# The MLP's input in one tile at an offset of its own, and a fifth room for the last gate's weight blocks

## The chip, the cores and the metric

The kernel runs on one core of one Trainium2 chip. The metric is the device time of one execution in microseconds; the median of three runs of the kernel before is 1739.65 us (1736.71 to 1743.08).

## The reference, cut to what matters

One layer of a diffusion backbone over 256 latent tokens and 256 context tokens of width 2048: an HGRN2 mixer, then a gated MLP with a width-3 convolution. The part that the change touches is the MLP on the latent tokens and the last of the six modulation vectors, the gate of the MLP:

```python
sh_ml, sc_ml, gt_ml, sh_fl, sc_fl, gt_fl = jnp.split((silu_c @ ada_w[i] + ada_b[i])[:, None, :], N_MOD, axis=-1)
h_l = modulate(rms_norm(x_lat, norm_ffn_pre[i]), sh_fl, sc_fl)
gate, up = jnp.split(h_l @ w_in, 2, axis=-1)          # 2048 -> 2 x 5632
f_l = (silu(dwconv_centred(gate, conv_w, conv_b)) * up) @ w_out
x_lat = x_lat + gt_fl * rms_norm(f_l, norm_ffn_post[i])
```

## The kernel before, in words

Every large product runs as three float32r matmuls (`mm3`, lines 200 to 202): an operand is split into a high part, rounded by a cast on ScalarE (line 106), and a low part, the difference, on VectorE (line 107). The three matmuls are high x high, high x low and low x high. The first operand of a matmul is stationary (its 128x128 block is loaded into TensorE), the second one moves past it, 256 or 512 columns at a time.

The weights stream through `Stream` (`ws`): blocks of 512 KB are loaded by SyncE's queue into four buffers `w_raw`, then split into three buffers each of `w_hi` and `w_lo`. A block of the MLP's first product has 4 x 2 stationary blocks, so it feeds 24 matmuls.

The stages in order: a start in which the modulation of the mixer is computed, the mixer's projections, its output product, a bridge in which the MLP's input is normed, turned and modulated, the MLP's first product with the convolution (22 steps of 8 weight blocks, lines 1063 to 1110), and the MLP's second product with the norm at its end.

The MLP's input is kept in 16 tiles, `h2h0` to `h2h7` (high parts) and `h2l0` to `h2l7` (low parts), each 128 partitions x 2 x 256 float32r, 2,048 bytes in a partition (lines 946 to 950). They move in the MLP's first product: one matmul reads one run of 256 numbers, 1,024 bytes, of one of them. The constant `SHIFT` (64) and the spacers of lines 531 and 947 place them: `w_hi` and `w_lo` start 64 bytes behind a multiple of 256 bytes of a partition, the `h2` tiles on a multiple of 256. In the mixer's projections with stationary weights the moving tiles `hTh`, `hTl` start on a multiple of 256 too; where the activations are stationary (the `v` projection and both output products) the weights move, and the moving side is the one 64 bytes behind. The tiles are filled by 8 casts and 8 subtractions (line 1062), and the first 64 float32 matmuls of the MLP (line 1077) read the unsplit copy `h2f`.

The last gate (`ada_part(5, ...)`, line 1058) needs a matrix-vector product with 2048 x 2048 numbers of `ada_w`. It is done beside the MLP's first 14 steps: 64 blocks of 256 KB are loaded by SyncE's queue (line 346) into a ring of `ADA_BUFS` = 4 tiles `ada_w`, and VectorE multiplies each by its number of the condition and adds it to one of four accumulators (lines 361 and 363). Three blocks are asked for ahead; after that each step of the generator asks for one more block and then uses one. The program places one such step per weight block, but the order of instructions on each engine is drawn up by the framework's planner, which fills idle time of its model with later work: the 64 loads are issued between 992.7 us and 1097.6 us of the span. VectorE and SyncE's queue run in that fixed order: a load of `ada_w` waits until its room is free (VectorE has used the block that lay there), a load of `w_raw` until the split of the block four earlier is done.

Of the kernel before, what the change touches and what calls it, by code (L numbers as in the profile page):

```python
# [8 lines left out]
F32 = mybir.dt.float32  # L9
F32R = mybir.dt.float32r  # L10
# [7 lines left out]
P = 128  # L18
D = 2048
KT = D // P  # L20
T = 256
# [8 lines left out]
MIX_RATE = 1.85  # L30
ADA_RATE = 3
ADA_BUFS = 4
ASIDE = 14


@with_exitstack
def tile_hgrn2_convffn_layer(
# [7 lines left out]
    ada_w, ada_b = ada_w[0], ada_b[0]  # L45
# [12 lines left out]
    def spacer(pool, nbytes):  # L58

        pool.tile([P, nbytes // 4], F32, name="spacer", bufs=1)  # L60
# [3 lines left out]
    SHIFT = 64  # L64
# [3 lines left out]
    def bank(pool, name):  # L68
        return pool.tile([P, 512], F32, name=name)
# [34 lines left out]
    def split(hi, lo, src):  # L104

        S.copy(out=hi, in_=src)  # L106
        V.tensor_tensor(out=lo, in0=src, in1=hi.bitcast(F32), op=ALU.subtract)  # L107

    class Stream:
# [37 lines left out]
        def next(self):  # L147
            self.ahead()
            got = self.done[self.pos]
            self.done[self.pos] = None  # L150
            self.pos += 1
            return got
# [186 lines left out]

    grow = {}  # L340

    def ada_part(part, pool):
        def loaded(i):
            b, r = divmod(i, KT)
            aw = pool.tile([P, 512], F32, name="ada_w", bufs=ADA_BUFS)
            nc.sync.dma_start(out=aw, in_=ada_w[r * P:(r + 1) * P, part * D + b * 512:part * D + (b + 1) * 512])
            return aw

        accs = []
        aws = [loaded(i) for i in range(ADA_BUFS - 1)]  # L350
        yield
        yield
        for b in range(4):
            acc = pool.tile([P, 512], F32, name="ada_acc", bufs=4)
            for r in range(KT):

                if len(aws) < 4 * KT:
                    aws.append(loaded(len(aws)))
                aw = aws[b * KT + r]
                if r == 0:  # L360
                    V.tensor_scalar(out=acc, in0=aw, scalar1=cst[:, r, 0:1], scalar2=None, op0=ALU.mult)
                else:
                    V.scalar_tensor_tensor(out=acc, in0=aw, scalar=cst[:, r, 0:1], in1=acc,  # L363
                                           op0=ALU.mult, op1=ALU.add)
                yield
            accs.append(acc)
        for _ in range(8):
            yield

        one = bank(ps_mi, "mi")  # L370
        for b in range(4):
            PE.matmul(out=one[32 * b:32 * b + 32, :], lhsT=ones32, rhs=accs[b], start=True, stop=True,
                      tile_position=(0, 32 * b), skip_group_check=True)
        strip_sb = pool.tile([P, 512], F32, name="ada_w", bufs=ADA_BUFS)
        S.copy(out=strip_sb, in_=one)
        for _ in range(4):
            yield
        if part in (3, 4):
            tp = bank(ps_mi, "mi")
            for i in range(4):  # L380
                PE.transpose(out=tp[:, i * P:(i + 1) * P], in_=strip_sb[:, i * P:(i + 1) * P], identity=ident)
            dst = shc_f if part == 3 else scc_f

            V.tensor_tensor(out=dst.rearrange("p (b i) -> p i b", i=4),
                            in0=tp.rearrange("p (i b r) -> p i b r", i=4, r=32)[:, :, :, 0],
                            in1=adab[:, part, :].rearrange("p (b i) -> p i b", i=4), op=ALU.add)
            if part == 4:
                V.scalar_tensor_tensor(out=scc_f, in0=scc_f, scalar=1.0, in1=g_ffn, op0=ALU.add, op1=ALU.mult)
        else:
            post = n_mix_post if part == 2 else n_ffn_post  # L390
            for w, src in enumerate((ada_b[part * D:(part + 1) * D], post[0])):
                gb = pool.tile([P, 512], F32, name="ada_acc", bufs=4)
                nc.gpsimd.memset(gb, 0.0)
                nc.sync.dma_start(out=gb[0::32, :], in_=src.rearrange("(b n) -> b n", b=4))
                V.tensor_tensor(out=strip_sb, in0=strip_sb, in1=gb, op=(ALU.add, ALU.mult)[w])
            gd = dram.tile([4, 512], F32, name=f"gd{part}")
            nc.sync.dma_start(out=gd, in_=strip_sb[0::32, :])
            grow[part] = gd
        yield
# [242 lines left out]
    def mixer():  # L642
        for p in range(NP):
            while "q" not in have.get(p, {}):
                yield
            yield from scan(p)
# [209 lines left out]
    def ada_rest():  # L856
        for part in (2, 3, 4):
            yield from ada_part(part, sp)

    ada, mix = ada_rest(), mixer()  # L860
# [66 lines left out]
    h2h, h2l, h2f, xin, hold = [], [], [], [], []  # L927

    def mixed():

        nonlocal h2
        with tc.high_priority(offset=200):
            split(zh[1], zl[1], z[1])
        for p in (*range(2, NP - 1), 0):
            split(zh[p], zl[p], z[p])
            for _ in range(MIXSTEP):
                next(mix, None)
            yield
        for _ in mix:
            pass  # L940
        split(zh[NP - 1], zl[NP - 1], z[NP - 1])
        yield
        yield
        zp_ctx.close()
        sp_ctx.close()
        h2 = h_ctx.enter_context(tc.tile_pool(name="h2", bufs=1))
        spacer(h2, 256 - SHIFT)
        for k in range(KT // 2):
            h2h.append(h2.tile([P, 2, T], F32R, name=f"h2h{k}"))
            h2l.append(h2.tile([P, 2, T], F32R, name=f"h2l{k}"))  # L950

        ws.early = early_ctx.enter_context(tc.tile_pool(name="early", bufs=1))
        for k4 in range(KT // 4):
            h2f.append(ws.early.tile([P, 4, T], F32, name=f"h2f{k4}"))

        xinp = xin_ctx.enter_context(tc.tile_pool(name="xinp", bufs=1))
        hold.append(xin_ctx.enter_context(tc.tile_pool(name="hold", bufs=MORE)))
        spacer(hold[0], SHIFT)
        for i in range(4):
            xin.append(xinp.tile([P, D // 2], F32, name=f"xin{i}"))  # L960
            nc.sync.dma_start(out=xin[i], in_=x[i // 2 * P:(i // 2 + 1) * P, i % 2 * 1024:(i % 2 + 1) * 1024])

    h2 = None
# [72 lines left out]
    def first_weights():  # L1036
        for _ in range(PLAIN):
            ws.prep()

    out_product(MIX_CHUNKS, list(zip(zh, zl)), grow[2], x1, yp, mix_eps, mix_done, 3 + MORE, mixed(), z0,  # L1040
                first_weights)

# [7 lines left out]
    def a_room(i0, i1, pool):  # L1050
        for i in range(i0, i1):
            a_hi.append(pool.tile([P, 2, T], F32R, name=f"ah{i}"))
            a_lo.append(pool.tile([P, 2, T], F32R, name=f"al{i}"))


    a_room(0, ASIDE, ap)
    gate_ctx = ExitStack()
    ada = ada_part(5, gate_ctx.enter_context(tc.tile_pool(name="gate", bufs=1, side="right")))
    for _ in range(LOOK):
        ws.prep()  # L1060
    for i in range(KT // 2):
        split(h2h[i], h2l[i], h2f[i // 2][:, i % 2 * 2:i % 2 * 2 + 2])
    for i in range(NFF):
        if i == ASIDE:
            for _ in ada:
                pass
            gate_ctx.close()
            a_room(ASIDE, NFF, ctx.enter_context(tc.tile_pool(name="ap2", bufs=1, side="right")))
        gu = []
# [84 lines left out]
```

## Time and profile before

| | us |
|---|---|
| median of three runs | 1739.65 |
| the profiled execution, its own time | 1740.89 |
| span of its instructions on the core | 1738.9 |
| TensorE matmuls busy | 1691.3 (97%) |
| TensorE weight loads busy | 1504.6 (87%) |
| VectorE busy | 1154.2 (66%) |
| ScalarE busy | 772.5 (44%) |
| MLP's first product with split operands, from its first to its last matmul | 1013.4 to 1489.7 |

The mean granted TensorE clock of the execution is 0.993 of full speed. A matmul's row in the profile is longer than the distance to the next one, since matmuls are pipelined: what a matmul costs in a stream is the distance from start to start, which the timeline gives.

### The profile page before, as it was taken

The numbers are of one execution on the slowest core, as the hardware profiler recorded it, in microseconds if no ns is written. First come the engines' busy times: TensorE is split into PE (matmuls) and PEld (weight loads), VectorE is DVE, ScalarE is ACT, GpSimd is POOL, SyncE is SP. The second block draws the span as 40 slices with busy tenths as digits, with TensorE's granted clock in tenths as the row PEclk, the third lists the DMA queues.
The fourth block names the chain that finished last, engine by engine and source line by source line (L and its number), as shares of the span: only waits on it lengthen the run. The fifth ranks groups of instructions, "written<-read, shape, count | busy, mean of one in ns | idle before, by whom it ended". The sixth has DMA issues, their size and how long they took to land.

```text
span 1738.9 us, 31985 instructions
## 1 busy us (share of the span) xinstructions
PE 1691.3 (97%) x12990; PEld 1504.6 (87%) x12990; DVE 1154.2 (66%) x1856; ACT 772.5 (44%) x1176; POOL 3.4 (0%) x13
## 2 busy tenths in 40 slices
PE   6999999899999999999999899999999999999998
PEld 4777888888989889898988799999999999888886
DVE  5777798865548875588565688766666666544444
ACT  4322264454545344443454544444444444443443
POOL 0000000000000000000000000000000000000000
PEclk9999999999999999999999999999999999999999
DMA  9897657633326863677348579766666666655654
GB/s 349 284 294 240 224 172 233 209 110 110 109 74 199 280 224 99 194 234 246 115 154 277 183 243 324 250 194 194 192 193 194 194 194 194 203 196 193 200 192 147
DMA packets 274646, 352.57 MB, mean 203 GB/s; under 512 B 12954, under 2 KB 197675, under 8 KB 273987
## 3 DMA queue, kind: packets, MB, share of 16 engines
q1 hardware_dynamic: 274499, 350.53, 62.5%
q8 instruction: 102, 1.67, 0.4%
q14 instruction: 45, 0.37, 0.1%
HBM read 348.37 MB, written 2.11 MB: 202 GB/s over the span
## 4 chain that ended last, share of the span: by engine, by line
PE 81%; DVE 8%; DMA 6%; issue 2%; ACT 1%; SPq 0%; DVEq 0%; ACTq 0%
PE pj L200 25%; PE pj L202 25%; PE pj L201 25%; DMA ada_w<-in_ada_w_dram 4%; DVE ada_acc L363 3%; DVE w_lo L107 2%; PE o L416 1%; ACT w_hi L106 1%; DVE k L692 1%; PE mi L804 1%; PE sc L732 1%; DMA w_raw<-in_hgrn_w_in_dram 1%; DMA aw<-in_ada_w_dram 1%; DMA hTh<-in_x_dram 0%; PE o L823 0%
## 5 line engine op out<-in xcount | busy, mean ns | idle before, releaser
L107 DVE TENSOR_TENSOR w_lo<-w_raw,w_hi 128x1024 fp32r<-128x1024 f32 x452 | 552.5, 1223 | 396.3 <-ACT w_hi L106 392.7
L106 ACT CAST w_hi<-w_raw 128x1024 fp32r<-128x1024 f32 x452 | 472.9, 1048 | 683.3 <-PE pj L201 367.9
L202 PE MATMUL pj<-h2h,w_lo 128*128 128x256 f32 x1376 | 381.0, 277 | 3.9 <-DVE w_lo L107 3.9
L200 PE MATMUL pj<-h2h,w_hi 128*128 128x256 f32 x1376 | 380.3, 276 | 0.0
L201 PE MATMUL pj<-h2l,w_hi 128*128 128x256 f32 x1376 | 380.0, 276 | 0.0
L200 PE MATMUL pj<-hTh,w_hi 128*128 128x256 f32 (+1 forms) x1040 | 353.2, 340 | 3.5 <-ACT w_hi L106 1.9
L202 PE MATMUL pj<-hTh,w_lo 128*128 128x256 f32 (+1 forms) x1040 | 348.0, 335 | 0.7 <-DVE w_lo L107 0.6
L201 PE MATMUL pj<-hTl,w_hi 128*128 128x256 f32 (+1 forms) x1040 | 348.2, 335 | 0.0
L202 PEld LDWEIGHTS pj<-h2h,w_lo 128*128 128x128 f32 x1376 | 258.4, 188 | 5.6 <-DVE w_lo L107 5.5
L200 PEld LDWEIGHTS pj<-h2h,w_hi 128*128 128x128 f32 x1376 | 258.3, 188 | 0.9 <-issue 0.8
L201 PEld LDWEIGHTS pj<-h2l,w_hi 128*128 128x128 f32 x1376 | 258.4, 188 | 0.0
L200 PEld LDWEIGHTS pj<-hTh,w_hi 128*128 128x128 f32 x1040 | 196.3, 189 | 33.7 <-issue 5.0
L202 PEld LDWEIGHTS pj<-hTh,w_lo 128*128 128x128 f32 x1040 | 196.3, 189 | 24.6 <-DVE w_lo L107 1.1
L201 PEld LDWEIGHTS pj<-hTl,w_hi 128*128 128x128 f32 x1040 | 196.7, 189 | 21.6 <-DVE hTl L107 0.2
L363 DVE SCALAR_TENSOR_TENSOR ada_acc<-ada_w,cst,ada_acc 128x512 f32<-128x512 f32 x240 | 179.7, 749 | 45.3 <-DMA ada_w<-in_ada_w_dram 42.2
L202 PE MATMUL pj<-w_hi,al 128*128 128x512 f32 x352 | 138.7, 394 | 0.0
L201 PE MATMUL pj<-w_lo,ah 128*128 128x512 f32 x352 | 138.0, 392 | 0.0
L200 PE MATMUL pj<-w_hi,hTh 128*128 128x256 f32 (+1 forms) x448 | 136.1, 304 | 0.6 <-DVE q L468 0.6
L200 PE MATMUL pj<-w_hi,ah 128*128 128x512 f32 x352 | 136.6, 388 | 0.0
L202 PE MATMUL pj<-w_hi,hTl 128*128 128x256 f32 (+1 forms) x448 | 134.0, 299 | 0.0
L201 PE MATMUL pj<-w_lo,hTh 128*128 128x256 f32 (+1 forms) x448 | 133.8, 299 | 0.0
L200 PEld LDWEIGHTS pj<-w_hi,hTh 128*128 128x128 f32 x448 | 85.9, 192 | 4.8 <-DVE stage L466 1.1
(226 smaller groups left out, 1792.1 us busy)
## 6 DMA issues: line engine op xcount, KB each, us to landing
w_raw<-in_ffn_w_in_dram SPq DMA_DIRECT2D x172, 512.0 KB, 3.9
w_raw<-in_hgrn_w_in_dram SPq DMA_DIRECT2D x160, 512.0 KB, 4.2
ada_w<-in_ada_w_dram SPq DMA_DIRECT2D x256, 256.0 KB, 4.0
w_raw<-in_ffn_w_out_dram SPq DMA_DIRECT2D x88, 512.0 KB, 3.6
aw<-in_ada_w_dram SPq DMA_DIRECT2D x64, 512.0 KB, 8.7
w_raw<-in_hgrn_w_out_dram SPq DMA_DIRECT2D x32, 512.0 KB, 4.2
hTh<-in_x_dram SPq DMA_DIRECT2D x2, 1024.0 KB, 4.9
hTh<-in_ctx_dram SPq DMA_DIRECT2D x2, 1024.0 KB, 10.3
```

Source lines behind the costliest of these rows:

```text
L106: S.copy(out=hi, in_=src)
L107: V.tensor_tensor(out=lo, in0=src, in1=hi.bitcast(F32), op=ALU.subtract)
L200: PE.matmul(out=o, lhsT=lh, rhs=rh, start=first, stop=False, skip_group_check=True)
L201: PE.matmul(out=o, lhsT=lh, rhs=rl, start=False, stop=False, skip_group_check=True)
L202: PE.matmul(out=o, lhsT=ll, rhs=rh, start=False, stop=last, skip_group_check=True)
L363: V.scalar_tensor_tensor(out=acc, in0=aw, scalar=cst[:, r, 0:1], in1=acc, op0=ALU.mult, op1=ALU.add)
L416: PE.matmul(out=strip[32 * a:32 * (a + 1), :], lhsT=cst[:, r4 * 4 + a, :], rhs=aws[r4][:, a].rearrange("p s n -> p (s n)"), start=(r4 == 0 ...
L692: V.tensor_tensor(out=half(t, i, m), in0=half(t, i, m), in1=half(by, 1 - i, m)[:, :, 0:1].to_broadcast([P, 256 // m, m]), op=ALU.mult)
L732: PE.matmul(out=o[32 * b:32 * b + 32, 32 * i:32 * i + 32], lhsT=flat(lhs[b % 2])[:, s0:s0 + 32], rhs=flat(rhs[b % 2])[:, t0:t0 + 32], star ...
L804: PE.matmul(out=sps[:, cs], lhsT=kT[:, d, h, ct], rhs=v[:, 2 + ct, h * P:(h + 1) * P], start=(ct == 0), stop=(ct == 1))
```

## The change

`ada_part` takes the number of rooms as an argument; the gate of the MLP gets five, the other parts keep four. The 16 tiles of the MLP's input become views of one tile `h2hl`, 192 bytes longer than the 16 together, as the spacer was; the first view starts 180 bytes into it, so that every view starts 12 bytes in front of a multiple of 256 bytes in its partition. The tiles behind it in the pool (`dg`, `cv`, `sg`) stay where they were. The pool of the gate grows by 2,048 bytes downwards, over memory that held the residual input `xin0` during the bridge.

```diff
+GATE_BUFS = 5
...
-    def ada_part(part, pool):
+    def ada_part(part, pool, bufs=ADA_BUFS):
         def loaded(i):
             b, r = divmod(i, KT)
-            aw = pool.tile([P, 512], F32, name="ada_w", bufs=ADA_BUFS)
+            aw = pool.tile([P, 512], F32, name="ada_w", bufs=bufs)
...
-        aws = [loaded(i) for i in range(ADA_BUFS - 1)]
+        aws = [loaded(i) for i in range(bufs - 1)]
...
-        strip_sb = pool.tile([P, 512], F32, name="ada_w", bufs=ADA_BUFS)
+        strip_sb = pool.tile([P, 512], F32, name="ada_w", bufs=bufs)
...
-        spacer(h2, 256 - SHIFT)
+
+        room = h2.tile([P, 48 + KT * 2 * T], F32R, name="h2hl")
+        at = (256 - 12 - SHIFT) // 4
         for k in range(KT // 2):
-            h2h.append(h2.tile([P, 2, T], F32R, name=f"h2h{k}"))
-            h2l.append(h2.tile([P, 2, T], F32R, name=f"h2l{k}"))
+            for part in (h2h, h2l):
+                part.append(room[:, at:at + 2 * T].rearrange("p (a t) -> p a t", a=2))
+                at += 2 * T
...
-    ada = ada_part(5, gate_ctx.enter_context(tc.tile_pool(name="gate", bufs=1, side="right")))
+    ada = ada_part(5, gate_ctx.enter_context(tc.tile_pool(name="gate", bufs=1, side="right")), GATE_BUFS)
```

## Rows read from the trace of the kernel before

**Rows 1.** The page: span, TensorE's busy time, chain that ended last by line.
```profile
span 1738.9 us, 31985 instructions
PE 1691.3 (97%) x12990; PEld 1504.6 (87%) x12990; DVE 1154.2 (66%) x1856; ACT 772.5 (44%) x1176; POOL 3.4 (0%) x13
...
PE pj L200 25%; PE pj L202 25%; PE pj L201 25%; DMA ada_w<-in_ada_w_dram 4%; DVE ada_acc L363 3%; DVE w_lo L107 2%; PE o L416 1%; ACT w_hi L106 1%; DVE k L692 1%; PE mi L804 1%; PE sc L732 1%; DMA w_raw<-in_hgrn_w_in_dram 1%; DMA aw<-in_ada_w_dram 1%; DMA hTh<-in_x_dram 0%; PE o L823 0%
```

**Rows 2.** Groups by line and form, MLP's first product: busy, mean, idle before.
```profile
L202 PE MATMUL pj<-h2h,w_lo 128*128 128x256 f32 x1376 | 381.0, 277 | 3.9 <-DVE w_lo L107 3.9
L200 PE MATMUL pj<-h2h,w_hi 128*128 128x256 f32 x1376 | 380.3, 276 | 0.0
```

**Rows 3.** Busy time by stretch: beside the gate, and behind it.
```profile
core 0: us, PE busy (x) PEld busy (x) DVE busy (x) ACT busy (x) POOL busy (x), PEclk, DMA share, GB/s
1020.00:1100.00 80.00, 76.25 (x654) 74.90 (x653) 72.86 (x97) 35.73 (x41) 0.00 (x0) 1.00 0.93 317
1300.00:1400.00 100.00, 100.00 (x884) 100.00 (x884) 62.18 (x70) 47.63 (x57) 0.00 (x0) 1.00 0.63 195
```

**Rows 4.** TensorE's timeline (start, duration), quiet stretch: starts nine matmuls apart.
```profile
1300.16 0.28 PE L200 MATMUL pj<-h2h,w_hi 128*128 128x256 f32 x1
...
1301.18 0.28 PE L200 MATMUL pj<-h2h,w_hi 128*128 128x256 f32 x1
```

**Rows 5.** The same beside the gate, after a wait: starts 57 matmuls apart.
```profile
1056.02 0.28 PE L200 MATMUL pj<-h2h,w_hi 128*128 128x256 f32 x1
...
1062.73 0.28 PE L200 MATMUL pj<-h2h,w_hi 128*128 128x256 f32 x1
```

**Rows 6.** The same, 512 columns: starts 3 apart (projection), 483 apart (second product).
```profile
105.03 0.39 PE L200 MATMUL pj<-hTh,w_hi 128*128 128x512 f32 x1
...
105.73 0.40 PE L200 MATMUL pj<-hTh,w_hi 128*128 128x512 f32 x1
...
1490.23 0.39 PE L200 MATMUL pj<-w_hi,ah 128*128 128x512 f32 x1
...
1600.78 0.39 PE L200 MATMUL pj<-w_hi,ah 128*128 128x512 f32 x1
```

**Rows 7.** The same: the plain float32 matmuls, then the first of the split product.
```profile
1003.02 10.74 PE L1077 MATMUL pj<-h2f,w_plain 128*128 128x256 f32 x49
1013.40 0.47 PE L200 MATMUL pj<-h2h,w_hi 128*128 128x256 f32 x1
```

**Rows 8.** TensorE's waits beside the gate; the last stands at 1104.92.
```profile
1046.59 0.39 PE L202 MATMUL pj<-h2h,w_lo 128*128 128x256 f32 x1 [1.41 <-DVE w_lo L107]
1064.81 0.38 PE L202 MATMUL pj<-h2h,w_lo 128*128 128x256 f32 x1 [0.63 <-DVE w_lo L107]
1087.97 0.39 PE L202 MATMUL pj<-h2h,w_lo 128*128 128x256 f32 x1 [1.11 <-DVE w_lo L107]
1104.92 0.39 PE L202 MATMUL pj<-h2h,w_lo 128*128 128x256 f32 x1 [0.18 <-DVE w_lo L107]
```

**Rows 9.** VectorE's timeline: the input's last splits; before the first two of those waits.
```profile
1003.63 2.49 DVE L107 TENSOR_TENSOR h2l<-h2f,h2h 128x512 fp32r<-128x512 f32 x4
...
1044.65 0.75 DVE L363 SCALAR_TENSOR_TENSOR ada_acc<-ada_w,cst,ada_acc 128x512 f32<-128x512 f32 x1 [1.38 <-DMA ada_w<-in_ada_w_dram]
1045.32 1.22 DVE L107 TENSOR_TENSOR w_lo<-w_raw,w_hi 128x1024 fp32r<-128x1024 f32 x1
...
1062.87 0.75 DVE L363 SCALAR_TENSOR_TENSOR ada_acc<-ada_w,cst,ada_acc 128x512 f32<-128x512 f32 x1 [1.54 <-DMA ada_w<-in_ada_w_dram]
```

**Rows 10.** SyncE's queue at the first of those waits.
```profile
1042.32 0.92 SPq L346 DMA_DIRECT2D ada_w<-in_ada_w_dram  x2
1046.57 0.38 SPq L126 DMA_DIRECT2D w_raw<-in_ffn_w_in_dram  x1
```

**Rows 11.** The tile `ada_w`, 985 to 1110 us: VectorE's waits, issue to landing.
```profile
  DMA ada_w<-in_ada_w_dram: 10.8, 15
DMA to landing us min/median/max: 2.6/4.4/5.7
```

## The prediction

> **What bounds the kernel now.** I read the page first: TensorE is busy 97% of the span, and the chain that ended last runs for three quarters over lines 200 to 202, the three matmuls of a split product [rows 1]. So time can come from two places only: the distance between matmuls, or gaps in TensorE's row. The groups by line and form say where the change acts: three lines of 1376 matmuls each, 4128 in all, read the input that is to be moved, and all their idle time, 3.9 us, stands in front of line 202 and is released by VectorE's `w_lo` [rows 2]. The stretches show two regimes. From 1020 to 1100 us, beside the gate, DMA engines are busy for 0.93 of the time and VectorE for 72.86 of 80 us; behind it DMA is at 0.63 and TensorE has no gap [rows 3].
>
> The timeline gives the price of a matmul. In the quiet stretch nine take 1.02 us, 113.3 ns each [rows 4]. [...] The same matmuls on the same tiles stand 6.71 us / 57 = 117.7 ns apart from 1056 to 1063 us, behind a wait of TensorE [rows 5]. [...]
>
> **The change part by part.** *The new offset.* No instruction is added or removed; the 4128 matmuls read their moving runs three columns (12 bytes) displaced against the stationary blocks. [...] I count it only for the quiet stretch, from TensorE's last wait at 1104.92 us [rows 8] to the stage's end at 1489.5: 384.6 us / 113.3 ns = 3390 matmuls, 13.6 us. Beside the gate each wait can leave another phase.
>
> The 16 instructions that fill the tiles now write displaced rows. The last four subtractions take 2.49 us and end at 1006.1 [rows 9]; the first matmul that needs them starts at 1013.40 [rows 7]. Under these 7.3 us even a doubling of all eight subtractions (5 us) stays hidden, and so would a first matmul that waits for the whole tile and not for its part. Without the cover, 5 us would be the price.
>
> *The fifth room.* Loads and multiplications stay 64 each, but a load may be issued one block earlier, on SyncE's queue past a multiplication that it waited for. TensorE stood still for 1.41 us before 1046.59 because `w_lo` came late [rows 8]; `w_lo` stood on VectorE behind a multiplication of the gate that had waited 1.38 us for its block [rows 9]. SyncE's queue closes the ring: behind two gate loads at 1042.32 it issued nothing until 1046.57 [rows 10], when that `w_lo` ended (1045.32 + 1.22) and freed a buffer `w_raw`, and the next gate loads waited too. The second long wait, 0.63 us, has the same forerunner, 1.54 us for a block [rows 8, 9]; a third, 1.11 us, I take for the same. What a perfect gate could give: from 1020 to 1100 us 652 matmuls start, two less than the row counts since two rows overlap its edge; at the quiet pace of 882 per 100 us it would be 705.6 [rows 3]; 53.6 x 113.3 ns = 6.1 us.
>
> VectorE waits 15 times for the gate's blocks, 10.8 us together, never over 1.54; a block lands 4.4 us after its issue [rows 9, 11]. The 64 loads take about 105 us, 1.6 us per block, so one block of lead covers nearly every such wait, if the DMA engines have the bandwidth. Bounds: 6.1 us gained; on the other side the planner, which now sees blocks arrive earlier, may crowd the gate's work, and two more waits like the longest cost 2.8 us. I take the three long waits as gone, 1.41 + 0.63 + 1.11 = 3.1 us. What is late next is `w_raw`, which shares the DMA engines.
>
> **Sum.** 1740.9 us (the profiled execution's own time: span 1738.9 and 2.0 around it) - 13.6 - 3.1 = 1724.2. The median of the runs lies 1.2 us below that execution: 1723.0. What a measurement of this kernel can tell from no change is about 0.3%, 5.2 us. The times below count from the median, too.
>
> **The rivals.** *No step* (0.32). All starts that the trace has lie on multiples of 64 bytes; perhaps 113.3 ns is what a run of 1,024 bytes costs, wherever it starts. For it: in the quiet stretch TensorE keeps its distance while VectorE and ScalarE come and go [rows 3, 4]. Against it: the dearer distance of the same tiles in rows 5, and the two distances of rows 6. Then the gate alone counts: 1739.7 - 3.1 = 1736.6, from 1733.6 with all 6.1 us to 1742.5 with two new waits.
>
> *The dearer phase* (0.14), which ends on the slower side. Its place is TensorE's last wait beside the gate: the phase that it leaves stays for 385 us. Before, 113.3 ns came out of it; at the new offset it may be the 117.7 ns of rows 5, 3390 x 4.4 ns = 14.9 us lost, 1751.5 with the gate's gain. It decides from that wait on.
>
> *A piece more* (0.09). If the moving run is fetched in pieces and their number sets the pace, a run that starts inside a piece needs one more. [...] Against it: by pieces alone, twice the columns would take twice 113.3 = 226.6 ns, and they take 228.9 and 233.3 [rows 6]. [...]
>
> **How the numbers follow.** The forecast has what is left, 0.45, a fifth of it for a step that only one or two of the three lines take (1727 to 1735). The low end is the step on all 4128 matmuls and a perfect gate: 1739.7 - 16.5 - 6.1 = 1717. The high end, 1745, takes in *no step* and *a piece more* up to the gate's doubt; the dearer phase and some of the tails stay outside. The forecast's own range is 1717 to 1735. Faster by over 0.3% (below 1734.4): the forecast, and a fifth of *no step*, 0.45 + 0.06 = 0.51. Slower (above 1744.9): the dearer phase and half of *a piece more*, 0.19 with rounding up. Within: the rest, 0.30.
>
> **What would show it.** [...] TensorE's idle time for `w_lo` between 1020 and 1110 us should fall below 1 us and VectorE's for the gate's blocks below 4; if both stay at a DMA share near 1, bandwidth sets the gate's pace and the room is worth nothing. I am wrong if the quiet distance is 113 ns or more: the gate alone passes 0.3% only if it becomes nearly perfect.

## The result, and the profile after

**The change made the kernel slower, by 1.2%.** The runs after have a median of 1762.88 us (four, 1761.0 to 1767.88), those before 1741.37 (four): ratio 1.012, 95% interval 1.0077 to 1.0162. The forecast was 1723.0, with a range up to 1745. The profiled execution took 1761.0 us.

From the page of the kernel after (span; the group behind [rows 2]; the chain that ended last). A line here is a number or four higher than before: L201 to L203 are the three matmuls, L108 the subtraction, L347 the gate's load, L364 its multiplication.

```profile
span 1759.2 us, 31972 instructions
...
L203 PE MATMUL pj<-h2hl,w_lo 128*128 128x256 f32 x1376 | 390.3, 284 | 0.8 <-DVE w_lo L108 0.8
L201 PE MATMUL pj<-h2hl,w_hi 128*128 128x256 f32 x1376 | 390.2, 284 | 0.0
...
PE pj L201 25%; PE pj L203 25%; PE pj L202 25%; DMA ada_w<-in_ada_w_dram 5%; DVE ada_acc L364 3%; DVE w_lo L108 2%; PE o L417 1%; PE sc L733 1%; ACT w_hi L107 1%; PE mi L805 1%; DVE k L693 1%; DMA aw<-in_ada_w_dram 1%; DMA hTh<-in_x_dram 0%; PE sc L1028 0%; DMA w_raw<-in_hgrn_w_in_dram 0%
```

The span is 20.3 us longer, the chain has the same shape, and TensorE's idle time for `w_lo` fell from 3.9 to 0.8 us. By idle time alone one would expect a faster kernel. The matmuls are what got longer, from 277 to 284 ns a row.

Busy time by stretch, kernel after (columns as in [rows 3]):

```profile
1020.00:1100.00 80.00, 79.15 (x648) 78.70 (x647) 72.08 (x96) 35.94 (x43) 0.00 (x0) 1.00 0.91 309
1300.00:1400.00 100.00, 100.00 (x836) 100.00 (x835) 58.62 (x65) 44.50 (x52) 0.00 (x0) 1.00 0.61 184
1600.00:1700.00 100.00, 100.00 (x438) 82.07 (x437) 47.16 (x41) 41.04 (x45) 0.00 (x0) 1.00 0.59 193
```

In the quiet stretch the count fell from 884 to 836 at the same granted clock, 1.00. Beside the gate TensorE is now busy for 79.15 of 80 us and yet starts fewer matmuls (648 for 654): a full row that does less.

TensorE's timeline, kernel after: the first split matmul, two nine apart in the quiet stretch, and the last of the product.

```profile
1009.63 0.47 PE L201 MATMUL pj<-h2hl,w_hi 128*128 128x256 f32 x1
...
1300.11 0.28 PE L201 MATMUL pj<-h2hl,w_hi 128*128 128x256 f32 x1
...
1301.19 0.28 PE L201 MATMUL pj<-h2hl,w_hi 128*128 128x256 f32 x1
...
1508.79 0.28 PE L203 MATMUL pj<-h2hl,w_lo 128*128 128x256 f32 x1
```

Nine matmuls take 1.08 us: 120.0 ns each, 113.3 before [rows 4]. That is 6.7 x 4128 = 27.5 us. The product lasts 499.2 us from its first to its last start, 476.0 before; of the 4.4 us between 27.5 and 23.1, TensorE's waits for `w_lo` explain 3.1 (3.9 before, 0.8 now); the rest, shorter gaps and changes of the distance beside the gate, was not taken apart. It also began 3.8 us earlier, at 1009.63 for 1013.40, with TensorE's instructions before it in the same order; the experiments' profiles scatter over as much there, so I give the change no credit for it. 23.1 - 3.8 = 19.3 of the 20.3 us; the stage behind keeps its pace (438 matmuls per 100 us; 439 in the kernel with four rooms below).

### The profile page after: what moved, and what is told of

Its sections match the earlier page's. It is cut to its first block, busy times and chain, and to the rows that moved or that the text cites. A ratio compares the mean times of both kernels' runs of the same rounds, so it can differ in the third digit from the quotient of the medians.

```text
span 1759.2 us, 31972 instructions
## 1 busy us (share of the span) xinstructions
PE 1713.4 (97%) x12990; PEld 1528.5 (87%) x12990; DVE 1154.0 (66%) x1856; ACT 772.4 (44%) x1176; POOL 3.4 (0%) x13
## 4 chain that ended last, share of the span: by engine, by line
PE 81%; DVE 8%; DMA 6%; issue 2%; ACT 1%; SPq 0%; DVEq 0%; ACTq 0%
PE pj L201 25%; PE pj L203 25%; PE pj L202 25%; DMA ada_w<-in_ada_w_dram 5%; DVE ada_acc L364 3%; DVE w_lo L108 2%; PE o L417 1%; PE sc L733 1%; ACT w_hi L107 1%; PE mi L805 1%; DVE k L693 1%; DMA aw<-in_ada_w_dram 1%; DMA hTh<-in_x_dram 0%; PE sc L1028 0%; DMA w_raw<-in_hgrn_w_in_dram 0%
## 5 line engine op out<-in xcount | busy, mean ns | idle before, releaser
L108 DVE TENSOR_TENSOR w_lo<-w_raw,w_hi 128x1024 fp32r<-128x1024 f32 x452 | 552.9, 1224 | 413.1 <-ACT w_hi L107 409.5
L203 PE MATMUL pj<-h2hl,w_lo 128*128 128x256 f32 x1376 | 390.3, 284 | 0.8 <-DVE w_lo L108 0.8
L201 PE MATMUL pj<-h2hl,w_hi 128*128 128x256 f32 x1376 | 390.2, 284 | 0.0
L202 PE MATMUL pj<-h2hl,w_hi 128*128 128x256 f32 x1376 | 389.9, 283 | 0.0
L201 PE MATMUL pj<-hTh,w_hi 128*128 128x256 f32 (+1 forms) x1040 | 352.4, 340 | 2.3 <-ACT hTh L107 1.6
L203 PE MATMUL pj<-hTh,w_lo 128*128 128x256 f32 (+1 forms) x1040 | 346.6, 334 | 1.5 <-DVE w_lo L108 1.4
L203 PEld LDWEIGHTS pj<-h2hl,w_lo 128*128 128x128 f32 x1376 | 261.5, 190 | 1.3 <-DVE w_lo L108 1.3
L201 PEld LDWEIGHTS pj<-h2hl,w_hi 128*128 128x128 f32 x1376 | 261.5, 190 | 0.9 <-issue 0.8
L202 PEld LDWEIGHTS pj<-h2hl,w_hi 128*128 128x128 f32 x1376 | 261.5, 190 | 0.0
L201 PEld LDWEIGHTS pj<-hTh,w_hi 128*128 128x128 f32 x1040 | 195.5, 188 | 32.5 <-issue 5.0
L203 PEld LDWEIGHTS pj<-hTh,w_lo 128*128 128x128 f32 x1040 | 195.4, 188 | 25.6 <-DVE w_lo L108 2.1
L364 DVE SCALAR_TENSOR_TENSOR ada_acc<-ada_w,cst,ada_acc 128x512 f32<-128x512 f32 x240 | 179.9, 750 | 45.0 <-DMA ada_w<-in_ada_w_dram 41.5
L203 PE MATMUL pj<-w_hi,al 128*128 128x512 f32 x352 | 138.7, 394 | 0.0
L201 PE MATMUL pj<-w_hi,ah 128*128 128x512 f32 x352 | 136.6, 388 | 0.0
L201 PE MATMUL pj<-w_hi,hTh 128*128 128x256 f32 (+1 forms) x448 | 135.0, 301 | 1.5 <-DVE q L469 0.8
L203 PE MATMUL pj<-w_hi,hTl 128*128 128x256 f32 (+1 forms) x448 | 132.8, 296 | 0.0
L201 PEld LDWEIGHTS pj<-w_hi,hTh 128*128 128x128 f32 x448 | 84.8, 189 | 5.6 <-DVE stage L467 1.8
```

The source lines that it names most:

```text
L201: PE.matmul(out=o, lhsT=lh, rhs=rh, start=first, stop=False, skip_group_check=True)
L202: PE.matmul(out=o, lhsT=lh, rhs=rl, start=False, stop=False, skip_group_check=True)
L203: PE.matmul(out=o, lhsT=ll, rhs=rh, start=False, stop=last, skip_group_check=True)
```

## The experiments

Two parts, two theories each: does the room or the slower TensorE end the waits, and what about the new start costs 6.7 ns? In the tables a distance in the quiet stretch comes from the row 1300 to 1400 us: 100 us by the count less two, as two matmuls overlap its edges.

### The parts one by one

**The fifth room alone.** The kernel before with `bufs` passed through as in the change, and the 16 tiles as they were:

```diff
+GATE_BUFS = 5
```

> The kernel before with the fifth room alone, the input in 16 tiles on multiples of 256 bytes. Theory A (pieces: a moving run is fetched in pieces of 64 bytes, and the distance between matmuls is 6.67 ns times one more than the pieces it touches) and theory B (the distance in bytes between moving and stationary operand sets it) both expect 113.3 ns from start to start in the quiet stretch of the MLP's first product. On the gate: if the room took the waits away (G1), TensorE waits for w_lo less than 1.5 us in all in that product and the time is 2 to 5 us below the kernel before; if it was the slower TensorE that gave the gate more time (G2), the waits are back at 3 to 4 us and the time is within 2 us of the kernel before.

Measured: 1741.0 us (median of 12) for 1740.17 (23), ratio 1.0012 (0.9985 to 1.0039). TensorE waits longer for `w_lo` than before, 5.3 us in five. The waits from 1009 to 1110 us, then VectorE's, SyncE's and TensorE's timelines at one of the two longest waits, 1.71 us (the longest is 1.75):

```profile
DVE ada_acc L364 <- DMA ada_w<-in_ada_w_dram: 10.2, 10, 2.6
...
PE pj L203 <- DVE w_lo L108: 5.3, 5, 1.8
```

```profile
1058.99 1.07 SPq L347 DMA_DIRECT2D ada_w<-in_ada_w_dram  x2
...
1062.44 0.75 DVE L364 SCALAR_TENSOR_TENSOR ada_acc<-ada_w,cst,ada_acc 128x512 f32<-128x512 f32 x1 [2.64 <-DMA ada_w<-in_ada_w_dram]
1063.11 1.22 DVE L108 TENSOR_TENSOR w_lo<-w_raw,w_hi 128x1024 fp32r<-128x1024 f32 x1
...
1064.35 0.38 SPq L127 DMA_DIRECT2D w_raw<-in_ffn_w_in_dram  x1
1064.38 0.39 PE L203 MATMUL pj<-h2h,w_lo 128*128 128x256 f32 x1 [1.71 <-DVE w_lo L108]
```

It is the ring of [rows 9, 10] again: two gate loads, a queue that then issues nothing until `w_lo` has freed a buffer `w_raw` at 1064.35, VectorE standing 2.64 us for a block of the gate with that `w_lo` behind it. One more block in front did not open it: VectorE's waits for blocks come to 10.2 us, 9.7 before. The ring is not the only candidate. While VectorE stood, the block was on its way and the DMA engines' share was 0.95 (columns as in [rows 3]):

```profile
1060.00:1062.00 2.00, 2.00 (x20) 2.00 (x19) 0.00 (x0) 0.69 (x1) 0.00 (x0) 1.00 0.95 324
```

In the kernel before their share was 1.03 from 1042 to 1044 us and 1.05 in the 2 us behind that, around the wait of VectorE in [rows 9]. Bandwidth, which the prediction had named as the other reason for a useless room, was not separated from the ring by any run. What the room does to the time can't be told from nothing. The first theory, that the room ended the waits, falls. For the second, that the slower TensorE did, the time fits and the waits are longer than the 3 to 4 us it had named.

**The new start alone**, with four rooms:

```diff
-GATE_BUFS = 5
+GATE_BUFS = 4
```

> The displaced input alone, the gate with four rooms. A and B: 120.0 ns from start to start, 4128 x 6.67 ns = 27.5 us more than before less what the gate's waits give back. G1 (the room took the waits away): TensorE's waits for w_lo in the MLP's first product stay at 3 us or more, so 25 to 28 us above the kernel before. G2 (the slower TensorE did): they fall below 1.5 us, and the time is about that of the changed kernel, 20 to 23 us above the kernel before.

Measured: 1765.61 us (median of 4), ratio 1.0124 (1.0084 to 1.0164): the whole loss. Two of its stretches:

```profile
1300.00:1400.00 100.00, 100.00 (x835) 100.00 (x835) 59.07 (x67) 44.95 (x52) 0.00 (x0) 1.00 0.59 182
...
1600.00:1700.00 100.00, 100.00 (x439) 82.04 (x438) 47.27 (x41) 40.90 (x45) 0.00 (x0) 1.00 0.57 192
```

The distance is 120.0 ns with four rooms too, and TensorE's waits for `w_lo` shrink to 1.9 us without a fifth. That lies between the two theories' figures, nearer to the second's, while the time, 25.4 us above the kernel before, is one that the first had named. The other profiles lean to the second. Between 1006 and 1120 us TensorE waits 3.9 to 5.9 us for `w_lo` in the five kernels whose matmuls stand 113.3 ns apart from 1120 to 1200 us, and 0.8 to 3.4 us in eight of the nine with 118 to 120 ns there (6.1 in the ninth, input 0 and weights 128 below). The reason that fits, not shown by a run of its own, is that a matmul that takes longer gives VectorE more time for each block of weights: 24 matmuls of 6.7 ns more are 0.16 us, by my estimate.

**The one tile alone**, starting on a multiple of 256, with five rooms:

```diff
-        at = (256 - 12 - SHIFT) // 4
+        at = (256 - SHIFT) // 4
```

> One tile and five rooms as in the changed kernel, but the input starts on a multiple of 256 bytes. If the offset is the cause (A, B): 113.3 ns from start to start and a time within 3 us of the run with the fifth room alone. If the one tile with its views is the cause: 120.0 ns and about 1762 us.

Measured: 1741.85 us (12), ratio 1.0002 (0.9978 to 1.0025).

```profile
1120.00:1200.00 80.00, 80.00 (x681) 80.00 (x680) 46.70 (x52) 35.79 (x41) 0.00 (x0) 1.00 0.61 188
1300.00:1400.00 100.00, 100.00 (x885) 100.00 (x884) 60.76 (x69) 47.52 (x55) 0.00 (x0) 1.00 0.63 193
...
1236.96 1.07 PE L373 MATMUL mi<-ada_acc,ones 128*32 128x512 f32 x8
```

113.3 ns in the stretch from 1300 us, and a time that can't be told from the kernel before: views of one tile cost nothing that shows. What is left is the start. From 1120 to 1200 us, though, the same matmuls on the same tiles stand 80.00 / 679 = 117.8 ns apart. They do so until the gate's eight last matmuls (the third row, from the timeline) break their stream, and behind these they stand 113.3 ns apart to the end. So one placement has two distances, the two of [rows 4, 5], and a break in the stream can change from one to the other. The run with fewer columns from the old start (below), the same program up to its step 14, has 113.3 ns on both sides of that break.

### Which starts are dear

**Four starts in one kernel**, two runs: each quarter of the 16 views, which a quarter of each step's matmuls read, gets its own. Those of the first run lie 128, 64, 32 and 16 bytes in front of a multiple of 256, those of the second 60, 12, 4 and 0.

```diff
-        at = (256 - 12 - SHIFT) // 4
+        at = 0
...
+            at += (64, 64, 32, 16)[k // 2] // 4 if k % 2 == 0 else 0
```

The second has `(132, 48, 8, 4)` there.

> The changed kernel with four offsets in one: the four tiles of each weight block's input start 128, 64, 32 and 16 bytes in front of a multiple of 256, for the first to fourth weight block of a step. Read in the quiet stretch, start to start, block by block. A (pieces of 64 bytes): 113.3, 113.3, 120.0, 120.0 ns. B (the distance to the stationary operand, 64 bytes before the change and 76 after it): four different values, or none of them 113.3 since none has the distance of 64. [...] Time by A: half of the changed kernel's loss, about 13 us above the kernel before.

> The same with starts 60, 12, 4 and 0 bytes in front of a multiple of 256 for the first to fourth block. A: 120.0, 120.0, 120.0, 113.3 ns; a start 4 bytes behind a multiple of 64 (the first block) costs as much as one 4 bytes in front of it. [...] B: values that rise or fall with the distance.

Measured: 1756.82 and 1762.27 us, 1745.88 before. Theory A misses the first set and comes within 2.5 ns of the second; B fits both, but it had asked for so little (no 113.3 in the first set, a rise or fall in the second) that this shows next to nothing. TensorE's timeline of the first, then of the second: the first matmul of four quarters and of the next one, 24 apart.

```profile
1300.47 0.28 PE L201 MATMUL pj<-h2hl,w_hi 128*128 128x256 f32 x1
...
1303.30 0.28 PE L201 MATMUL pj<-h2hl,w_hi 128*128 128x256 f32 x1
...
1306.14 0.28 PE L201 MATMUL pj<-h2hl,w_hi 128*128 128x256 f32 x1
...
1308.96 0.28 PE L201 MATMUL pj<-h2hl,w_hi 128*128 128x256 f32 x1
...
1311.82 0.28 PE L201 MATMUL pj<-h2hl,w_hi 128*128 128x256 f32 x1
```

```profile
1304.39 0.28 PE L201 MATMUL pj<-h2hl,w_hi 128*128 128x256 f32 x1
...
1307.33 0.29 PE L201 MATMUL pj<-h2hl,w_hi 128*128 128x256 f32 x1
...
1310.22 0.29 PE L201 MATMUL pj<-h2hl,w_hi 128*128 128x256 f32 x1
...
1313.09 0.28 PE L201 MATMUL pj<-h2hl,w_hi 128*128 128x256 f32 x1
...
1315.83 0.28 PE L201 MATMUL pj<-h2hl,w_hi 128*128 128x256 f32 x1
```

The first run's quarters take 2.83, 2.84, 2.82 and 2.86 us: 118 to 119 ns for every start. The second run's take 2.94, 2.89, 2.87 and 2.74: 122.5, 120.4, 119.6 and, back on the multiple of 256, 114.2. Even 4 bytes cost nearly the whole step, and so do 64, so whether the run starts inside a piece of 16, 32 or 64 bytes is not what decides. But mixing starts may mislead: the start at 128, alone, takes 113.3 or 117.8 ns below, so its 117.9 here may be that second distance, kept on from the quarter before it.

**Fewer columns** from the displaced start: step by step 256, 244, 242 and 226, by which the end of the run comes back over a multiple of 64 bytes. It leaves the last tokens out of most of the sum.

```diff
+                        n = (256, 244, 242, 226)[i % 4] if kt else T
```

> The changed kernel, input displaced by 12 bytes, but the matmuls of the MLP's first product move 256, 244, 242 and 226 columns in steps 0, 1, 2, 3 and so on in turn (the first of the 16 blocks of the contraction keeps 256): the last tokens are left out of most of the sum. A: these runs touch 17, 17, 16 and 15 pieces of 64 bytes, so 120.0, 120.0, 113.3 and 106.7 ns: two columns less, from 244 to 242, take 6.7 ns away, twelve less, from 256 to 244, nothing. [...]

Measured: 1778.83 us, with 28.2 us of waits of its own for `w_lo` beside the gate, where the granted clock fell to 0.79 (1020 to 1100 us); the stretch read here has it at 1.00. TensorE's timeline: the first matmul of steps 13 to 17 (244, 242, 226, 256 and again 244 columns), 192 apart, 12 of them on 256 columns in any step.

```profile
1328.15 0.28 PE L201 MATMUL pj<-h2hl,w_hi 128*128 128x256 f32 x1
...
1350.00 0.28 PE L201 MATMUL pj<-h2hl,w_hi 128*128 128x256 f32 x1
...
1371.84 0.28 PE L201 MATMUL pj<-h2hl,w_hi 128*128 128x256 f32 x1
...
1393.37 0.28 PE L201 MATMUL pj<-h2hl,w_hi 128*128 128x256 f32 x1
...
1416.41 0.28 PE L201 MATMUL pj<-h2hl,w_hi 128*128 128x256 f32 x1
```

244 columns take 21.85 / 192 = 113.8 ns, 242 take 113.7, 226 take 112.1 and 256 take 120.0. Between 244 and 242 there is no step, so where the run ends on the grid of 64 bytes is not the price; and something else stops the fall at 112.

**Fewer columns from the old start**, on a multiple of 256: 256 up to step 14, then 240, 192, 128 in turn; again it leaves tokens out.

```diff
-        at = (256 - 12 - SHIFT) // 4
+        at = (256 - SHIFT) // 4
...
+                        n = (240, 192, 128)[i % 3] if kt and i > 14 else T
```

> The input on a multiple of 256; from step 15 on the matmuls of the MLP's first product move 240, 192 or 128 columns in turn (all but the first block of the contraction), so the last tokens are left out of most of the sum there. If the moving run sets the distance (A, or a price by column): 106.7, 86.7, 60.0 ns by pieces, or 106.7, 86.7, 60 by column. D, with the weight load as a second bound: the distance stays near 110 ns from 240 columns down to 128, as the 111.6 ns of 226 displaced columns already hint.

Measured: 1740.31 us (1738.84 before). The first matmul of steps 15 to 18:

```profile
1336.06 0.28 PE L201 MATMUL pj<-h2hl,w_hi 128*128 128x256 f32 x1
...
1357.73 0.28 PE L201 MATMUL pj<-h2hl,w_hi 128*128 128x256 f32 x1
...
1379.22 0.30 PE L201 MATMUL pj<-h2hl,w_hi 128*128 128x256 f32 x1
...
1400.70 0.33 PE L201 MATMUL pj<-h2hl,w_hi 128*128 128x256 f32 x1
```

240 columns: 21.67 us, 112.9 ns. 192: 111.9. 128: 21.48 us, 111.9. With half the columns a matmul starts no earlier. Each comes with the load of a stationary block of 128 columns, and that doesn't change (884 loads for 884 matmuls in the row of 1300 to 1400 us in [rows 3]): that about 112 ns is the pace of the weight loads is my estimate, and no run changed the load to show it. If the floor is the same at other starts, which no run tried, the most that any start of the input could have given is 113.3 - 111.9 = 1.4 ns, 6 us over 4128.

### Place or distance

The weights start 64 bytes behind a multiple of 256. So the change took the distance between the two starts from 64 bytes to 76. Is it the input's own place that costs, or its place against the weights? First the input alone, five rooms, 64 and 128 bytes in front of the multiple of 256, and 192, which is where the weights start:

```diff
-        at = (256 - 12 - SHIFT) // 4
+        at = (256 - 64 - SHIFT) // 4
```

> One tile, five rooms, the whole input 64 bytes in front of a multiple of 256, on the same place within 256 bytes as a displacement of the stationary operand by 128. Theory A, mended (the run of four offsets mixed its blocks, and the blocks on multiples of 64 inherited a phase from their neighbours): 113.3 ns in the quiet stretch. Theory D (the moving read and the weight load run beside each other through the same memory; where both start decides how often one holds the other up, so there are good and bad places and no rule by multiples): a value of its own, near the 118.8 ns of that block.

> The same 128 bytes in front. A, mended: 113.3 ns. D: near the 117.8 ns that this block had among the four offsets; should it be 113.3 alone, the 117.8 was an inherited phase, and this one case goes to A.

> One tile, five rooms, the input 192 bytes in front of a multiple of 256, so on the very place within 256 bytes on which the split weights start (64 behind). P (the moving run's own place counts: 0 and 128 behind a multiple of 256 are free, 192 costs 118.7 ns): 64 is free too, as where the weights move in the projections, 113.3 ns in the quiet stretch. Q (the distance between moving and stationary start counts: 64 either way is free, 128 costs 118.7 ns): distance 0, not measured so far; if the two reads meet in one place, 117 ns or more.

Then the weights, four rooms: `w_hi` and `w_lo` become views of one tile each, `WOFF` in front of their old place (12 is place 52; 192 is place 128), with the input at 0, or at its own new place. The mixer's weights lie in the same tiles and move along, so these six runs also differ before the MLP: their split product begins at 1013.2 to 1019.5 us, in the other profiles at 1006.9 to 1013.7.

```diff
+                    at = 64 - WOFF // 4 + self.turn * 1024
+                    self.turn = (self.turn + 1) % 3
+                    hi, lo = (r[:, at:at + 1024].rearrange("p (a n) -> p a n", a=a) for r in self.rooms)
```

> The input on a multiple of 256, the split weights 12 bytes in front of their old place, four rooms. If only the moving read's own place counts (A): 113.3 ns in the MLP's first product, and one step more in the second product, where the weights move, as with both displaced (233.4 ns). D: the first product leaves 113.3 ns too, though no moving run was touched there.

> Input and split weights both 12 bytes in front of their old places, the distance of 64 bytes between them kept, four rooms. A: 120.0 ns in the MLP's first product, and every stage in which the weights move pays one piece more per matmul too: 228.9 becomes 235.6 ns in the MLP's second product (1056 matmuls, 7.0 us), 8 to 11 us more than the displaced input alone in all. B: 113.3 ns and 228.9 ns, the time of the kernel before.

> The input on a multiple of 256, the split weights 128 behind one, four rooms: distance 128 with the moving run on its good place. P: 113.3 ns in the quiet stretch. Q: 118.7 ns.

> The input 64 bytes in front of a multiple of 256, where it cost 118.7 ns, the split weights moved along so that they start 64 in front of it (distance 64), four rooms. P: 118.7 ns again. Q: 113.3 ns.

> Four rooms; the split input starts 64 bytes behind a multiple of 256, the weights of the MLP 128 bytes behind one: the distance is 64 again, as in the kernel before, on multiples of 64. Theory Q (the distance between the two starts decides, 64 is cheap, with 113.3 ns or, in its dearer phase, 117.8): 113.3 ns from start to start in the quiet stretch, or 117.8 throughout if this run falls into the dearer phase. Theory W (weights 128 bytes behind a multiple of 256 are dear themselves, wherever the input lies): 118.7. Theory O (both own places count: 64 is a dear place of the input, as at 120.0 with the weights at 64): 120.0 or more.

> Four rooms; input and weights both start 128 bytes behind a multiple of 256: distance 0. Theory Q: 120.0 ns in the quiet stretch, as with both at 64. Theory W: 118.7, as with the input at 0 and the weights at 128. Theory O (128 is a cheap place of the input): 118.7 as well.

Measured (places are bytes behind a multiple of 256, "apart" is the shorter way round these 256; a count off by one is 0.14 ns; the times are single runs but for the first and the last line, to be held against a run of before of 1738.84, where marked * 1745.88, ** 1744.63; 23 runs of before on one chip lay between 1734 and 1756, so the distances tell more than the times):

| input | weights | apart | us | ns, quiet |
|---|---|---|---|---|
| 0 | 64 | 64 | 1741.37 | 113.3 |
| 128 | 64 | 64 | 1745.87 | 113.3 |
| 192 | 64 | 128 | 1754.86 | 118.6 |
| 64 | 64 | 0 | 1759.17 | 120.0 |
| 64 | 128 | 64 | 1749.64** | 113.3 |
| 192 | 128 | 64 | 1765.63 | 117.8 |
| 0 | 128 | 128 | 1771.85 | 118.6 |
| 128 | 128 | 0 | 1775.12** | 119.9 |
| 0 | 52 | 52 | 1751.32 | 113.3 |
| 244 | 52 | 64 | 1767.29* | 119.3 |
| 244 | 64 | 76 | 1762.88 | 119.9 |

The rows by stretch behind it, one kernel a fence, in the order input and weights at 128/64, 192/64, 64/64, 64/128, 192/128, 0/128, 128/128, 0/52, 244/52:

```profile
1300.00:1400.00 100.00, 100.00 (x885) 100.00 (x884) 60.76 (x69) 47.46 (x55) 0.00 (x0) 1.00 0.62 193
```

```profile
1300.00:1400.00 100.00, 100.00 (x845) 100.00 (x844) 58.20 (x65) 44.62 (x51) 0.00 (x0) 1.00 0.61 185
```

```profile
1300.00:1400.00 100.00, 100.00 (x835) 100.00 (x835) 58.61 (x65) 44.89 (x52) 0.00 (x0) 1.00 0.60 184
```

```profile
1300.00:1400.00 100.00, 100.00 (x885) 100.00 (x884) 61.32 (x68) 47.14 (x55) 0.00 (x0) 1.00 0.62 195
```

```profile
1300.00:1400.00 100.00, 100.00 (x851) 100.00 (x851) 60.24 (x68) 46.25 (x54) 0.00 (x0) 1.00 0.60 185
```

```profile
1300.00:1400.00 100.00, 100.00 (x845) 100.00 (x845) 59.67 (x68) 46.09 (x54) 0.00 (x0) 1.00 0.59 185
...
1600.00:1700.00 100.00, 100.00 (x432) 81.09 (x431) 45.11 (x39) 39.02 (x40) 0.00 (x0) 1.00 0.56 191
```

```profile
1300.00:1400.00 100.00, 100.00 (x836) 100.00 (x835) 58.57 (x67) 45.34 (x53) 0.00 (x0) 1.00 0.58 182
```

```profile
1300.00:1400.00 100.00, 100.00 (x885) 100.00 (x884) 61.07 (x68) 47.11 (x55) 0.00 (x0) 1.00 0.63 194
...
1600.00:1700.00 100.00, 100.00 (x429) 80.27 (x428) 46.49 (x40) 39.61 (x44) 0.00 (x0) 1.00 0.56 190
```

```profile
1300.00:1400.00 100.00, 100.00 (x840) 100.00 (x839) 59.39 (x66) 45.38 (x54) 0.00 (x0) 1.00 0.60 184
```

On multiples of 64 the number of bytes between the two starts decides, in all eight pairs. 0 apart costs 120 ns and 128 apart 118.6, whichever place the weights have. 64 apart costs 113.3, or the 117.8 of [rows 5]. No place is dear by itself: the input at 64 gives 120.0 or 113.3, at 128 it gives 113.3 or 119.9, at 0 113.3 or 118.6; so the theories by which the input's own place counts, or the weights', fell. The run at 192/128 has 117.8 in the quiet stretch, where the distance theory had said 113.3 and that of own places 118.7. Its own timeline settles it: behind a wait beside the gate, 45 matmuls stand 5.10 / 45 = 113.3 ns apart.

```profile
1050.17 0.28 PE L210 MATMUL pj<-h2hl,w_hi 128*128 128x256 f32 x1
...
1055.27 0.28 PE L210 MATMUL pj<-h2hl,w_hi 128*128 128x256 f32 x1
```

In the profiles every pair 64 apart on the grid has both prices somewhere in the MLP's first product, and no stretch of over 20 matmuls of a pair 128 or 0 apart came below 118. That 64 apart has two prices is in the mixer of the kernel before as well, where weights at 64 move over activations at 0. TensorE's timeline of before, in two of the mixer's projections, 24 matmuls apart each:

```profile
541.11 0.28 PE L200 MATMUL pj<-w_hi,hTh 128*128 128x256 f32 x1
...
543.94 0.28 PE L200 MATMUL pj<-w_hi,hTh 128*128 128x256 f32 x1
...
749.06 0.28 PE L200 MATMUL pj<-w_hi,hTh 128*128 128x256 f32 x1
...
751.78 0.28 PE L200 MATMUL pj<-w_hi,hTh 128*128 128x256 f32 x1
```

2.83 / 24 = 117.9 ns the one time, 2.72 / 24 = 113.3 the other. Between two breaks of TensorE's stream (a matmul that starts over 0.15 us after the one before) the price holds, for over 2000 matmuls at the longest; it changes at breaks, as at the eight matmuls of the gate in the run of the one tile, and at 128/64, which stood at 117.8 up to the same break and at 113.3 behind it. What at a break picks the one or the other was not found.

Off the multiples of 64 the distance is not enough: 244 and 52 are 64 apart and cost 119.3, 0 and 52 cost 113.3. There the displaced *input* is dear, displaced weights are not in the quiet stretch (beside the gate 0/52 has stretches at 117.8 and 120.0, too); in the second product, where these same weights move, they are dear too. It fell from 439 to 429 matmuls per 100 us, 5.4 ns each by the counts, 5.7 us over its 1056. In these runs a run that started off the grid cost when it moved. The start of the change itself, 244/64, has a second distance as well: in the kernel after, 48 matmuls from 1069.79 to 1075.71 us stand 123.3 ns apart. Moving weights at 128, on the grid, cost there as well (432): against activations on a multiple of 256 they are 128 apart, the dear distance of the first product.

The total times hold these second costs: the kernel with 64/128 has the cheap distance and is still 5.0 us behind its kernel before, 3.7 of them in the second product (245.2 us from first to last start, 241.5 before). No version here beats the kernel before; the two nearest, the fifth room alone and the one tile at its old place, can't be told from it.

## Why the prediction was wrong, point by point

- **"I count it only for the quiet stretch ... 3390 matmuls, 13.6 us."** This step failed, in its direction. The 13.6 us of the sum and the 16.5 us of the low end are both 4.0 ns off each matmul, and no run shows these 4.0 ns: at the old start the distance fell by 1.4 ns, to 111.9, even with half the columns. So as far as that floor holds the gain had room for 6 us, not 16.5. And the price went up: 6.7 ns x 4128 = 27.5 us, where the sum had -13.6. Nor is there one step of about 4 ns: the quiet stretches show 113.3, 117.8, 118.6, 119.3 and 120.0.
- **"... it may be the 117.7 ns of rows 5."** As the dearest price of a matmul it failed too: the quiet stretches went up to 120.0. I took it from the dearest distance that the trace of before had for these tiles. But all pairs of split operands in that trace are 64 apart: it could show the two prices of that distance, and none of 0, 128 or a start off the grid. An unknown start was not bounded by rows that all share one.
- **Three long waits gone, 3.1 us.** Failed. The lead of one block was to cover VectorE's waits for the gate's blocks, "if the DMA engines have the bandwidth"; it doesn't: five rooms alone leave 5.3 us of TensorE's waits and 10.2 of VectorE's, and in the kernel after VectorE's stay at 9.7. Whether the ring or the bandwidth holds the blocks back is open. That the kernel after waits 0.8 us for `w_lo`, below the 1 us that was to show a hit, is luck: it goes with the slower TensorE, as four rooms with the new start have 1.9.
- **The rivals.** *No step* is excluded by the run of the new start alone. *The dearer phase* had the sign and fell short: 4.4 ns from the last wait on, where 6.7 came with every matmul of the quiet stretch and most of those before it. The phase itself is real: the one tile at the old start kept 117.8 ns from wait to break. *A piece more* had the direction; no run shows what a piece would cost, and the new start cost 6.7 ns. Its mechanism falls, since a start on the grid, with no piece more, cost as much: with the weights at 64, a run from 64 took 120.0 ns against 113.3 from 0.
- **The range's high end**, 1745, left the dearer phase outside and had nothing beyond it.
- Right: nothing else moved that shows (the second product's pace, the splits under their cover, the one tile for nothing), the quiet stretch's distance was the place to look, and its sign of being wrong, 113 ns or more there, came.

## What to carry to other kernels

Where every matmul comes with a new stationary block, place the moving and the stationary tile against each other, not each by itself: here 64 bytes apart on multiples of 64 gave 113.3 ns per 256 float32r columns, or 117.8 behind some breaks of the stream, and every other pair on that grid 118.6 to 120.0; keep the moving run on the grid. Take a price for an untried placement from a run that tries it. And read the distance from start to start: a TensorE whose waits vanish while its row stays full may just have become slower.

## What the runs showed of the hardware that I had not expected

The relative place of the moving and the stationary operand in a partition cost 5.3 to 6.7 ns per matmul here (113.3 against 118.6 and 120.0). That the moving read and the weight load hold each other up is my guess; no run watches the reads themselves. What the runs show is that neither place decides alone: with the input at 0, weights moved from 64 to 128 take the distance from 113.3 to 118.6 ns; with the input at 64 the same move takes it from 120.0 to 113.3. What sets the price of a distance, what picks the second price of 117.8, and the rule for starts off the grid are open.
